# Weight sums of the second FFN product in two tiles, one filled by a copy, and DVE and ACT in text order through pairs and second product

## The chip, the core and the metric

The kernel runs on one core of a Trainium2 chip. The metric is the device time of one execution in microseconds (us). The engines that matter here: PE multiplies matrices, DVE and ACT do elementwise work, POOL issues some of the DMAs, SP issues the others. Each engine runs its instructions one after the other in the order in which they stand in its own stream; between engines, semaphores make one wait for another.

## The reference, cut to what matters

A decoder trunk of two layers in float32 on 512 tokens of width 1024. Each layer is a mixer and a feed-forward net (FFN) of width 4096 with squared ReLU:

```python
def sqrelu_mlp(x, w1, w2):
    return jnp.square(jax.nn.relu(x @ w1)) @ w2
...
    for l in range(DEPTH):
...
        x = layer_norm(DEEPNORM_ALPHA * x + mix, ln_mix_g[l], ln_mix_b[l])
        x = layer_norm(DEEPNORM_ALPHA * x + sqrelu_mlp(x, ffn_w1[l], ffn_w2[l]), ln_ffn_g[l], ln_ffn_b[l])
```

The mixers (differential and block-sparse attention in layer 0, gated linear attention in layer 1) and the norms are not touched by the change.

## The kernel before, in words

**Precision.** A float32 product is made of three products of rounded halves: each operand `v` is split into `h` (rounded copy, made by ACT, L117) and `l = v - h` (made by DVE, L118), and PE adds `h·h`, `h·l` and `l·h`. So each weight that arrives costs one ACT and one DVE instruction before PE can use it, and each step of a product is three matmuls.

**Blocks.** `ffn()` walks over the 4096 FF columns in four blocks of 1024. In each block the first matrix is done unit by unit or by pairs of units (`pair`, L872): block 0 has six plain units and one pair, blocks 1, 2 and 3 have four pairs each. Blocks 0 to 2 then multiply by their part of W2 at once (`second`, L927); block 3 is handled apart. So each layer has 13 pairs and three calls of `second`, the core 26 and six.

**A pair** replaces eight products of quarter size by seven: `b11`, `t1`, `t2`, `b21`, `t3`, `b22`, `t4`, each of 12 matmuls of 128x256 (L881), into three banks `ba`, `bb`, `bc`. Some banks are read in between and then accumulated on: ACT copies `ba` out after `b11` (`p1`, L892), `bc` after `t1` (`p5`, L896), `ba` again after `t2` (`u2`, L900). DVE then forms `c11 = p1 + bb`, `c22 = p5 + ba` (after `t3`) and `c12 = u2 + bc`, all at L815. The product `t4` accumulates on `ba`, so it may not start before `c22` has read it. Last, ACT applies ReLU and square (L914, L828, L916, L917, L828) into `hb`.

**The weights of a pair** are five entries made by `add_pair`: `first` (1024 columns), `s1` and `s2` (512), `s3` (1024), `s4` (512). `s1` is a DVE sum (L194) of a fresh load, `s2`, `s3`, `s4` are DVE subtractions (L187); each is then split. `done` hands slots back after a product and calls `pump(2)`, which writes the next entries into the text at that place.

**The second product** does seven products of 24 matmuls of 128x512 (L944) into six banks: A, C and B. Its left operands are sums of the block's activations, split into tiles `ho` by `left`. Each finished partial result is added to `x` by DVE (`into_x`, L403 and L405). Its right operands are quarters of W2: some plain loads (`raw`), some sums of two or three quarters in two `ws` tiles, built by DMAs that POOL issues (L225, and L230 for those that add to what is there).

**What sets the order.** A scheduler decides the order of each engine's stream from the program's text and its dependencies; the DMA issues of `ws` are kept in program order. The names `raw` (four buffers, loaded over SP's queue), `w` (split weights), `pp` and `pf` (PSUM banks of the first and second matrix) are those in the rows below.

Of the kernel before, what the change touches and what calls it, by code (L numbers as in the profile page):

```python
# [19 lines left out]
P = 128  # L20
# [27 lines left out]
def trunk(ctx, tc, a, out):  # L48
# [164 lines left out]
    def quad(u, i, n, half):  # L213

        return wst[u + 4 * i + 2 * n + half]
# [3 lines left out]
    def start_sums(key):  # L219

        u = blocks[key]
        tsum[key] = [t8("ws", (P, 2, 1024)) for _ in range(2)]
        for t, i in zip(tsum[key], (0, 1)):
            for half in range(2):
                tc.keep_in_program_order(nc.gpsimd.dma_start(t[:, half], quad(u, 0, 1, half)))  # L225
            for half in range(2):
                add_quad(t[:, half], quad(u, i, i, half))

# [5 lines left out]
    def add_block(u, key):  # L234
# [10 lines left out]
        def summed(m, then=None):  # L245
            def fn(half, h, l):
                t = tsum[key][m][:, half]
                split(h, l, t)
                if then:
                    add_quad(t, quad(u, *then, half))  # L250
            return [(len(loads), 2, lambda h, l, half=half: fn(half, h, l)) for half in range(2)]

        steps = (lambda: plain(0, 0), lambda: summed(0, (1, 1)), lambda: plain(1, 0), lambda: plain(1, 1),
                 lambda: summed(0, (1, 0)), lambda: summed(1), lambda: summed(0))
        return [e for st in steps for e in st()]
# [556 lines left out]
    def ffn(layer, last, nfirst, c0, t_last):  # L812
# [114 lines left out]
        def second():  # L927
# [43 lines left out]
            V.scalar_tensor_tensor(s, s, -1.0, a11, op0=ALU.mult, op1=ALU.subtract)  # L971
            V.scalar_tensor_tensor(a12, a12, -1.0, s, op0=ALU.mult, op1=ALU.subtract)
            prod("C", o1, True)
            into_x(1, 1, c["C"])
            o4 = left(a12)
            c["B"] = [bank("pf") for _ in range(2)]
            prod("B", o12, True)
            into_x(0, 0, c["B"])
            o2 = left(s)
            sub(a21, a11, a21)  # L980
            prod("C", o4, False)
            into_x(0, 1, c["C"])
            o3 = left(a21)
            prod("A", o2, False, True)
            into_x(0, 1, c["A"])
            o22 = left(a22)
# [11 lines left out]
        for b in range(NB):  # L998
# [10 lines left out]
            if b == 0:  # L1009
                third()  # L1010
            for n in range(PLAIN[b], FBLK, 2):
                pair(n // 2, ops_)
            if not fin:
                second()
                continue
# [398 lines left out]
```

## Time and profile before

| | us |
|---|---|
| median of 3 runs | 1190.36 |
| lowest, highest | 1188.38, 1193.89 |
| the profiled execution | 1192.47 |
| its span in the trace | 1190.7 |
| PE busy in it | 1140.6 (96%) |
| DVE busy | 867.8 (73%) |
| ACT busy | 622.8 (52%) |
| POOL busy | 112.2 (9%) |

The mean granted clock of TensorE in this execution is 0.992 of full speed. A busy PE is not PE at its peak: the records of matmuls overlap. So the idle time of PE, and what ended it, are what to read; the view of waits gives them by place, and the chain of work that ended last tells where the end of the execution hangs on something other than PE.

### The profile page before, as it was taken

Reading aid. Unit: us, or ns where it says so; the run is one execution under the profiler, and the core shown is the slowest. Engines: PE = TensorE matmul, PEld = TensorE weight load, DVE = VectorE, ACT = ScalarE, POOL = GpSimd, SP = SyncE. Lnnn points to the kernel's source line nnn. Section 1 sums busy time; section 2 is a strip of 40 time slices with the busy share of each in tenths; the row PEclk is TensorE's granted clock in tenths of the full one; section 3 lists DMA queues with packets and bytes.
Section 4 is the critical chain, followed back from the end, with each engine's and each line's share of the span. In section 5 each row is a group of like instructions: output and inputs, shape, how many; then the busy total and the mean of one; then the engine's idle time right before and its main releaser. Section 6 shows DMA issues by size and latency. Waiting matters only on the chain.

```text
span 1190.7 us, 16757 instructions
## 1 busy us (share of the span) xinstructions
PE 1140.6 (96%) x6538; PEld 988.1 (83%) x6538; DVE 867.8 (73%) x1359; ACT 622.8 (52%) x1046; POOL 112.2 (9%) x136
## 2 busy tenths in 40 slices
PE   9999999999989999999999999999999899899997
PEld 6787776889779789799888888888987887887986
DVE  5677863578976986995657756486879679679846
ACT  6535466446646647566336433633564565564731
POOL 1132410010110010001010000000102002000000
PEclk9999999999999999999999999999999999899998
DMA  7512242073674675435232123401656566463331
GB/s 265 205 53 71 71 147 66 1 212 94 139 210 121 141 200 142 107 106 188 72 102 84 58 87 99 138 32 50 181 159 161 140 163 174 125 168 66 121 107 71
DMA packets 42735, 145.79 MB, mean 122 GB/s; under 512 B 5152, under 2 KB 6176, under 8 KB 42656
## 3 DMA queue, kind: packets, MB, share of 16 engines
q1 hardware_dynamic: 30640, 101.92, 26.3%
q0 software_dynamic: 12016, 42.80, 16.5%
q8 instruction: 51, 0.84, 0.3%
q14 instruction: 28, 0.23, 0.1%
HBM read 142.61 MB, written 2.10 MB: 122 GB/s over the span
## 4 chain that ended last, share of the span: by engine, by line
PE 79%; DVE 6%; ACT 6%; issue 4%; DMA 3%; POOL 1%; DVEq 0%; POOLq 0%; ACTq 0%
PE pp L881 20%; PE pf L944 15%; PE pf L280 4%; PE pf L279 4%; PE pf L281 4%; PE pb L279 4%; PE pb L280 4%; PE pb L281 3%; PE pa L279 3%; PE pa L281 3%; PE pa L280 3%; DMA raw<-in_wst 3%; ACT w L117 2%; DVE w L118 2%; PE pl L1212 1%
## 5 line engine op out<-in xcount | busy, mean ns | idle before, releaser
L118 DVE TENSOR_TENSOR w<-raw,w 128x1024 fp32r<-128x1024 f32 (+2 forms) x210 | 242.6, 1165 | 122.5 <-ACT w L117 99.4
L117 ACT ACTIVATE w<-raw 128x1024 fp32r<-128x1024 f32 (+2 forms) x210 | 205.7, 986 | 167.1 <-PE pf L944 26.9
L944 PE MATMUL pf<-w,ho 128*128 128x512 f32 x1008 | 234.9, 391 | 4.9 <-ACT ho L117 4.0
L944 PEld LDWEIGHTS pf<-w,ho 128*128 128x128 f32 x1008 | 187.4, 188 | 48.0 <-ACT ho L117 6.6
L881 PE MATMUL pp<-xTh,w 128*128 128x256 f32 x832 | 161.3, 286 | 9.3 <-ACT w L117 5.8
L881 PEld LDWEIGHTS pp<-xTh,w 128*128 128x128 f32 x832 | 135.6, 194 | 12.1 <-ACT w L117 7.5
L881 PE MATMUL pp<-T,w 128*128 128x256 f32 x936 | 127.1, 289 | 14.9 <-DVE hb L815 14.9
L881 PEld LDWEIGHTS pp<-T,w 128*128 128x128 f32 x936 | 119.2, 196 | 16.8 <-DVE hb L815 15.7
L881 PE MATMUL pp<-xTl,w 128*128 128x256 f32 x416 | 118.9, 286 | 0.0
L279 PE MATMUL pa<-xTh,w 128*128 128x512 f32 x264 | 106.0, 403 | 0.0
L281 PE MATMUL pa<-xTh,w 128*128 128x512 f32 x264 | 103.1, 391 | 0.0
L280 PE MATMUL pa<-xTl,w 128*128 128x512 f32 x264 | 103.0, 390 | 0.0
L881 PEld LDWEIGHTS pp<-xTl,w 128*128 128x128 f32 x416 | 81.0, 195 | 0.2
L230 POOL DMA_DIRECT2D ws<-in_wst x48 | 42.1, 877 | 400.5 <-DVE w L118 334.8
L279 PE MATMUL pb<-w,xTh 128*128 128x512 f32 x192 | 76.3, 401 | 1.0 <-ACT w L117 1.0
L280 PE MATMUL pb<-w,xTh 128*128 128x512 f32 x192 | 75.1, 391 | 0.4 <-DVE w L118 0.4
L281 PE MATMUL pb<-w,xTl 128*128 128x512 f32 x192 | 75.3, 392 | 0.0
L117 ACT ACTIVATE w<-ws 128x1024 fp32r<-128x1024 f32 x48 | 50.8, 1059 | 42.4 <-PE pf L944 41.6
L118 DVE TENSOR_TENSOR w<-ws,w 128x1024 fp32r<-128x1024 f32 x48 | 58.1, 1220 | 14.0 <-ACT w L117 9.2
L281 PEld LDWEIGHTS pa<-xTh,w 128*128 128x128 f32 x264 | 49.6, 188 | 10.6
L280 PEld LDWEIGHTS pa<-xTl,w 128*128 128x128 f32 x264 | 49.8, 188 | 9.2
L279 PEld LDWEIGHTS pa<-xTh,w 128*128 128x128 f32 x264 | 49.7, 189 | 9.1
(280 smaller groups left out, 2082.5 us busy)
## 6 DMA issues: line engine op xcount, KB each, us to landing
raw<-in_wst SPq DMA_DIRECT2D x178, 512.0 KB, 3.6
ws<-in_wst POOLq DMA_DIRECT2D x72, 512.0 KB, 6.0
xraw<-in_xT SPq DMA_DIRECT2D x8, 256.0 KB, 4.9
x<-in_x SPq DMA_DIRECT2D x4, 512.0 KB, 6.8
gb<-in_lng POOLq DMA_DIRECT2D x4, 512.0 KB, 5.6
gb<-in_lnb POOLq DMA_DIRECT2D x4, 512.0 KB, 6.5
out_x<-x SPq DMA_DIRECT2D x7, 256.0 KB, 2.0
tab<-in_rope SPq DMA_DIRECT2D x2, 512.0 KB, 5.2
```

The costliest lines, as they stand in the source:

```text
L117: A.activation(h, src, AF.Copy)
L118: V.tensor_tensor(l, src, h.bitcast(F32), op=ALU.subtract)
L230: tc.keep_in_program_order(nc.gpsimd.dma_start(t, src, accum_op=ALU.add))
L279: PE.matmul(o, l[0], r[0], start=first, stop=False)
L280: PE.matmul(o, l[0], r[1], start=False, stop=False)
L281: PE.matmul(o, l[1], r[0], start=False, stop=last)
L881: PE.matmul(o, w[x_], z[y_], start=first and k == n == 0, stop=k == 3 and n == 2, skip_group_check=True)
L944: PE.matmul(c[k][tt], l[x_], r[y_][:, j, :], start=first and half == j == n == 0, stop=half == j == 1 and n == 2, skip_group_check=True)
L1212: PE.matmul(pl[:, h * P:(h + 1) * P], z, z, start=True, stop=True)
```

## The change

First, the two `ws` sums of a block. Before, tile 0 went through three contents (Q01+Q00, then +Q11, then +Q10) and tile 1 held Q01+Q11. Now `a1` = Q01+Q00 and `a2` starts as a copy of `a1`, made by a DMA between tiles, +Q11. After `a1` is split, it is filled anew (Q01, then +Q11); after `a2` is split, Q10 is added to it. POOL issues 14 DMAs for each block where it issued 12. Second, the products of `second` come in another order: A(Q00), C(`a1`), B(Q10), A(`a2`), C(Q11), A(`a1` anew), A(`a2`+Q10), and the left operands are formed in the order that goes with it. Third, the pairs and `second` of all blocks are put under a manual schedule for DVE and ACT: these two engines run that part in the order of the text, while PE, SP and POOL are still ordered as before.

```diff
--- before.py
+++ after.py
@@ -219,12 +219,18 @@
     def start_sums(key):
 
         u = blocks[key]
-        tsum[key] = [t8("ws", (P, 2, 1024)) for _ in range(2)]
-        for t, i in zip(tsum[key], (0, 1)):
-            for half in range(2):
-                tc.keep_in_program_order(nc.gpsimd.dma_start(t[:, half], quad(u, 0, 1, half)))
-            for half in range(2):
-                add_quad(t[:, half], quad(u, i, i, half))
+        a1, a2 = tsum[key] = [t8("ws", (P, 2, 1024)) for _ in range(2)]
+        for half in range(2):
+            bring(a1[:, half], quad(u, 0, 1, half))
+        for half in range(2):
+            add_quad(a1[:, half], quad(u, 0, 0, half))
+        for half in range(2):
+            bring(a2[:, half], a1[:, half])
+        for half in range(2):
+            add_quad(a2[:, half], quad(u, 1, 1, half))
+
+    def bring(t, src):
+        tc.keep_in_program_order(nc.gpsimd.dma_start(t, src))
 
     def add_quad(t, src):
         tc.keep_in_program_order(nc.gpsimd.dma_start(t, src, accum_op=ALU.add))
@@ -247,11 +253,16 @@
                 t = tsum[key][m][:, half]
                 split(h, l, t)
                 if then:
-                    add_quad(t, quad(u, *then, half))
+                    then(t, half)
             return [(len(loads), 2, lambda h, l, half=half: fn(half, h, l)) for half in range(2)]
 
-        steps = (lambda: plain(0, 0), lambda: summed(0, (1, 1)), lambda: plain(1, 0), lambda: plain(1, 1),
-                 lambda: summed(0, (1, 0)), lambda: summed(1), lambda: summed(0))
+        def third(t, half):
+            bring(t, quad(u, 0, 1, half))
+            add_quad(t, quad(u, 1, 1, half))
+
+        steps = (lambda: plain(0, 0), lambda: summed(0, third), lambda: plain(1, 0),
+                 lambda: summed(1, lambda t, half: add_quad(t, quad(u, 1, 0, half))),
+                 lambda: plain(1, 1), lambda: summed(0), lambda: summed(1))
         return [e for st in steps for e in st()]
 
     def add_ffn(u, layer):
@@ -969,20 +980,20 @@
             into_x(0, 0, c["A"])
             o12 = left(a12)
             V.scalar_tensor_tensor(s, s, -1.0, a11, op0=ALU.mult, op1=ALU.subtract)
-            V.scalar_tensor_tensor(a12, a12, -1.0, s, op0=ALU.mult, op1=ALU.subtract)
             prod("C", o1, True)
             into_x(1, 1, c["C"])
-            o4 = left(a12)
+            V.scalar_tensor_tensor(a12, a12, -1.0, s, op0=ALU.mult, op1=ALU.subtract)
+            o2 = left(s)
             c["B"] = [bank("pf") for _ in range(2)]
             prod("B", o12, True)
             into_x(0, 0, c["B"])
-            o2 = left(s)
+            o4 = left(a12)
             sub(a21, a11, a21)
+            prod("A", o2, False)
+            into_x(0, 1, c["A"])
+            o3 = left(a21)
             prod("C", o4, False)
             into_x(0, 1, c["C"])
-            o3 = left(a21)
-            prod("A", o2, False, True)
-            into_x(0, 1, c["A"])
             o22 = left(a22)
             prod("A", o3, False, True)
             into_x(1, 1, c["A"])
@@ -1008,10 +1019,12 @@
             fill.drain()
             if b == 0:
                 third()
-            for n in range(PLAIN[b], FBLK, 2):
-                pair(n // 2, ops_)
+            with tc.manual_schedule(engines={mybir.EngineType.DVE, mybir.EngineType.Activation}):
+                for n in range(PLAIN[b], FBLK, 2):
+                    pair(n // 2, ops_)
+                if not fin:
+                    second()
             if not fin:
-                second()
                 continue
             gb = load_gb(2 * layer + 1)
             W["un"] = 2
```

The streams of three engines show what moves. In these rows the numbers behind names are those of buffers; `w` are split weights, `s` and `raw` the unsplit sums and loads, `hb` the activations, `p1`, `p5`, `u2` the copies out of PSUM. Line 815 of before is 826 of the changed kernel, 881 is 892, and so on.

**DVE, block 1 of layer 0, second pair** (before, from the sum `s_3388` of the pair after the next to that pair's `c11`, `c22`, `c12`):

```order
L194 TENSOR_TENSOR s_3388<-raw_3123 128x512
L187 TENSOR_TENSOR raw_3040<-raw_3040,s_3261 128x512
L118 TENSOR_TENSOR w_3301<-s_3261,w_3301 128x512
L187 TENSOR_TENSOR raw_3123<-raw_3121,raw_3123 128x512
L118 TENSOR_TENSOR w_3332<-raw_3042,w_3331 128x1024
L118 TENSOR_TENSOR w_3336<-raw_3040,w_3336 128x512
L815 TENSOR_TENSOR hb_3132<-p1_3273,pp_3271 128x256
L815 TENSOR_TENSOR hb_3133<-p5_3274,pp_3270 128x256
L815 TENSOR_TENSOR hb_3132<-u2_3275,pp_3272 128x256
```

The same place in the changed kernel (raw_3044 and raw_3046 are this one's loads for the third pair, `hb_3137` and `hb_3138` the activations):

```order
L194 TENSOR_TENSOR s_3268<-raw_3046 128x512
L118 TENSOR_TENSOR w_3267<-s_3268,w_3267 128x512
L187 TENSOR_TENSOR s_3268<-s_3268,raw_3044 128x512
L118 TENSOR_TENSOR w_3308<-s_3268,w_3308 128x512
L187 TENSOR_TENSOR raw_3046<-raw_3044,raw_3046 128x512
L118 TENSOR_TENSOR w_3339<-raw_3046,w_3338 128x1024
L187 TENSOR_TENSOR raw_3044<-raw_3044,s_3268 128x512
L118 TENSOR_TENSOR w_3343<-raw_3044,w_3343 128x512
L826 TENSOR_TENSOR hb_3137<-p1_3280,pp_3278 128x256
L826 TENSOR_TENSOR hb_3138<-p5_3281,pp_3277 128x256
L826 TENSOR_TENSOR hb_3137<-u2_3282,pp_3279 128x256
```

In both, the `s3` and `s4` weights of the next loads are split ahead of `c11`, `c22` and `c12`. Before, the subtractions for them stand well ahead and the two splits follow each other; now the subtraction of `s4` (`raw_3044`) stands between the split of `s3` and that of `s4`, and the sum of a later pair (`s_3395<-raw_3127`) that stood ahead now comes behind `c12`.

**PE, the same pair** (before, the end of `t1`, then `t2` and the start of what follows it):

```order
L881 MATMUL pp_3272<-T_2573,w_3125 128x256 x12
L881 MATMUL pp_3270<-T_2574,w_3175 128x256 x12
L881 MATMUL pp_3271<-xTh_1707,w_3117 128x256
L881 MATMUL pp_3271<-xTl_1708,w_3117 128x256
L881 MATMUL pp_3271<-xTh_1707,w_3118 128x256
```

and in the changed kernel, `t2` and what follows it:

```order
L892 MATMUL pp_3277<-T_2574,w_3182 128x256 x12
L892 MATMUL pp_3279<-xTh_1707,w_3217 128x256
L892 MATMUL pp_3279<-xTl_1708,w_3217 128x256
L892 MATMUL pp_3279<-xTh_1707,w_3217 128x256 x2
L892 MATMUL pp_3277<-xTh_1707,w_3212 128x256
L892 MATMUL pp_3277<-xTl_1708,w_3212 128x256
```

`T_2574` is the right operand of `t2`. Before, `t2` is followed by the 12 matmuls of `b21` (`pp_3271`), 12 of `t3` and 12 of `b22`, and then by `t4`: 36 matmuls. Now `b21` stands ahead of `t2`, and between `t2` and `t4` lie 12 of `t3`, 12 of `b22` and four of later pairs: 28.

**ACT, the end of block 1 of layer 0** (before, from the last pair's ReLU to the operands of `second`; one half of `ho_3642` stands much earlier, in the third pair):

```order
L117 ACTIVATE w_3628<-raw_3383 128x1024
L914 ACTIVATE hb_3132<-hb_3132 128x2x256
L917 ACTIVATE hb_3133<-pp_3516 128x256
L828 ACTIVATE hb_3132<-hb_3132 128x2x256
L828 ACTIVATE hb_3133<-hb_3133 128x2x256
L117 ACTIVATE ho_3642<-hb_3132 128x512
L117 ACTIVATE w_3666<-raw_3385 128x1024
L117 ACTIVATE ho_3650<-s_3648 128x1024
```

and in the changed kernel:

```order
L117 ACTIVATE w_3637<-raw_3390 128x1024
L925 ACTIVATE hb_3137<-hb_3137 128x2x256
L839 ACTIVATE hb_3137<-hb_3137 128x2x256
L927 ACTIVATE hb_3138<-hb_3138 128x256
L928 ACTIVATE hb_3138<-pp_3523 128x256
L839 ACTIVATE hb_3138<-hb_3138 128x2x256
L117 ACTIVATE ho_3651<-hb_3137 128x512 x2
L117 ACTIVATE ho_3659<-s_3657 128x1024
```

Both halves of the first left operand (`ho_3651`) now stand together, behind the last pair's square of `hb_3138`, with the split of a raw weight (`w_3637`) ahead of the ReLU.

## Rows read from the trace of the kernel before

**Rows 1.** The page's chain that ended last: shares of the span by engine.

```profile
PE 79%; DVE 6%; ACT 6%; issue 4%; DMA 3%; POOL 1%; DVEq 0%; POOLq 0%; ACTq 0%
```

**Rows 2.** View of waits, PE, whole span: engine, line <- releaser: total us, times, longest.

```profile
PE pp L881 <- DVE hb L815: 14.9, 4, 4.3
PE pp L881 <- ACT w L117: 5.8, 4, 1.5
PE pf L944 <- ACT ho L117: 4.0, 6, 0.8
...
PE pp L881 <- DVE w L118: 3.5, 2, 1.7
...
PE pf L944 <- DVE ho L118: 0.6, 4, 0.2
```

**Rows 3.** The chain in order of time: start, us, engine and line, matmuls.

```profile
352.01 33.58 PE pp L881 x263
...
438.41 32.08 PE pp L881 x263
...
934.40 33.66 PE pp L881 x263
...
1022.13 34.50 PE pp L881 x263
```

**Rows 4.** Timeline, 344 to 352.5 us, DVE and PE: start, us, operation, [idle before <-releaser].

```profile
347.67 0.69 DVE L194 TENSOR_TENSOR s<-raw 128x512 f32<-128x512 f32 x1 [4.55 <-DMA raw<-in_wst]
...
352.01 2.93 PE L881 MATMUL pp<-T,w 128*128 128x256 f32 x12 [4.32 <-DVE hb L815]
```

**Rows 5.** Timeline where the second product of block 0 starts (PE, ACT), and 366.45 (ACT).

```profile
297.43 2.91 PE L944 MATMUL pf<-w,ho 128*128 128x512 f32 x12
...
297.51 1.06 ACT L117 ACTIVATE w<-raw 128x1024 fp32r<-128x1024 f32 x1 [1.89 <-PE pp L881]
...
298.48 0.61 ACT L914 ACTIVATE hb<-hb 128x512 f32<-128x512 f32 x1
...
299.00 0.37 ACT L917 ACTIVATE hb<-pp 128x256 f32<-128x256 f32 x1
...
300.30 0.62 ACT L117 ACTIVATE ho<-hb 128x512 fp32r<-128x512 f32 x1
...
366.45 0.62 ACT L117 ACTIVATE ho<-hb 128x512 fp32r<-128x512 f32 x1
```

**Rows 6.** Timeline, 359 to 365 us, a pair of block 1: ACT, DVE and PE.

```profile
359.35 0.38 ACT L900 ACTIVATE u<-pp 128x256 f32<-128x256 f32 x1 [0.54 <-PE pp L881]
...
359.62 1.79 ACT L117 ACTIVATE w<-raw 128x1024 fp32r<-128x1024 f32 x2
...
360.74 1.83 DVE L118 TENSOR_TENSOR w<-raw,w 128x1024 fp32r<-128x1024 f32 x2 [0.87 <-ACT w L117]
...
362.48 0.74 DVE L815 TENSOR_TENSOR hb<-p,pp 128x256 f32<-128x256 f32 x2
...
363.46 1.60 PE L881 MATMUL pp<-T,w 128*128 128x256 f32 x12
```

**Rows 7.** Groups by form, 352 to 390 us: xcount | busy us, mean ns of one.

```profile
L118 DVE TENSOR_TENSOR w<-raw,w 128x1024 fp32r<-128x1024 f32 x7 | 8.6, 1224 | 7.9 <-ACT w L117 4.1 <-PE pp L881 3.8
...
L916 ACT ACTIVATE hb<-hb 128x256 f32<-128x256 f32 x4 | 1.7, 417 | 6.6 <-DVE hb L815 6.6
...
L118 DVE TENSOR_TENSOR w<-raw,w 128x512 fp32r<-128x512 f32 x2 | 1.4, 688 | 1.2 <-ACT w L117 1.2
...
L187 DVE TENSOR_TENSOR raw<-raw,s 128x512 f32<-128x512 f32 x2 | 1.4, 682 | 0.0
L117 ACT ACTIVATE w<-raw 128x512 fp32r<-128x512 f32 x2 | 1.3, 627 | 0.1
```

**Rows 8.** Stretch table, PE: stretch, us, busy (instructions), granted clock, DMA share, GB/s.

```profile
352.00:354.00 2.00, 1.99 (x9) 0.50 0.94 305
```

**Rows 9.** The page's DMA issues: count, KB each, median us from issue to landing.

```profile
ws<-in_wst POOLq DMA_DIRECT2D x72, 512.0 KB, 6.0
```

## The prediction

> **What bounds the kernel now.** I read the chain that ended last first: 79% of it is PE [rows 1], so only what changes PE's idle time or its clock counts. Then the view of waits: in the FFN, PE stands still at two kinds of seam [rows 2]. At the six exits from `second` into the next block's pairs (three in each layer) it waits for DVE's L815 (14.9 us) and for freshly split weights (5.8 and 3.5): together 24.2. At the six starts of `second` it waits 4.0 + 0.6 for `ho`, or 0.77 each time. The reader is to see why an exit waits: PE's `t4` of a first pair begins at 352.01 after 4.32 us of idle time that L815 ended, and L815 stood in DVE's stream behind L194, the sum of a later pair, which had waited 4.55 us for its load [rows 4]. Inside a pair, PE does not wait: `u2` starts at 359.35 as `t2` ends, `c11` and `c22` end at 363.22, and `t4` follows at 363.46 with no idle time, behind 36 matmuls that kept PE busy [rows 6]. That is a narrow escape: the chain takes 3.9 us from `u2`'s start and 36 matmuls cover 36 x 0.122 = 4.4 (263 in 32.08 us at full clock [rows 3]).
>
> **Exits, removed: -24.2.** In the new DVE stream `c11`, `c22`, `c12` of a first pair stand ahead of the later pair's L194, so the wait for that load no longer holds them; the split weights of the first pair come first too. I take all 24.2 away. What is late next there is the pair's own chain, costed below, so nothing is counted as covered by it.
>
> **Starts of `second`, added: +20.0.** Before, one half of the first `ho` is split in the middle of a pair (366.45 in block 1), so PE goes on at once, at 297.43 in block 0 [rows 5]. Now both halves stand behind the last pair's tail. From the end of `t4` (T = 297.43) ACT runs the split of a raw weight, ReLU, `c21` and two squares, and reaches the second half of `ho` at 300.30, ending 0.62 later: T + 3.49 [rows 5]. The new stream has one more instruction there, ReLU of `c22`, 0.42 [rows 7] less some 0.09 by which neighbours' records overlap: T + 3.82. PE then has two matmuls before it needs the `l` half, which DVE gives 0.69 later [rows 7]: about 0.25 more. So 4.1 instead of 0.77, six times: 6 x 3.33 = 20.0. Bounds: 6 x 2.7 = 16 if the raw split ahead finds its slot early and is done by then; 6 x 3.7 = 22 if hand-overs cost as much as the 0.1 seen between T and 297.51.
>
> **Pairs, added: +43.3.** This is the large term. In the new DVE stream `c11` stands behind the `s4` weight of the next pair, and the way to it now goes back and forth: `u2` (0.38 [rows 6]), split of `s3` on ACT (1.06 [rows 5]), its `l` on DVE (1.22), the subtraction for `s4` on DVE (0.68), its split on ACT (0.63), its `l` (0.69) [rows 7], then `c11` and `c22` (0.74 [rows 6]). The sum is 5.40; records of neighbours on one engine overlap by some 0.1 and hand-overs cost about as much, so I keep 5.2 to 5.5. Before, the subtraction stood ahead and the two splits ran side by side on both engines, which is why the chain took 3.9. At the same time the cover shrinks: 28 matmuls instead of 36, 28 x 0.122 = 3.4 us. PE should wait 5.4 - 3.4 = 2.0 us at `t4`. Laid out instruction by instruction with these durations, the waits at `t4` are, in block 1: 0.6 for the first pair (24 matmuls of the last `second` product lie in between), 1.9, 2.1, 0.3 (the last pair of a block has no weights of a next one to split); in block 2: 2.2, 1.9, 2.1, 0.3; in block 3, where two splits follow each square: 2.6, 0.4, 2.8, 0.3. That is 17.5 a layer. Beside it, once in block 1 and once in block 2, the `first` weight of a later pair gets its slot only when `t4` ends, and PE's next product waits for its split and its `l`: 1.06 + 1.22 less two matmuls, 2.05 and 2.1. Together 21.65 a layer, 43.3 for two. Bounds: with every overlap of 0.1 counted and no hand-over, the chain is 4.8 and the long waits are 1.4: 0.7 of the sum, 30. With hand-overs of 0.1 at each of the four changes of engine and no overlap, 5.8: 2.4, or 52.
>
> **The last product, added: +3.3.** `o22` writes the bank that `into_x` of the product before it has to read, and this now stands in text order behind the next weights on DVE. The next pair's 48 matmuls cover most of it; I lay out 0.55 left, six times. Bounds 0 and, with one more 1.22 split ahead [rows 7], 7.
>
> **The sums in `ws`: 0.** The second contents are now formed by two transfers one behind the other instead of one, but the products that use them come later. By 6.0 us a transfer [rows 9] the later half of `a1` anew lands 17.5 us after T and is split from 23.7 on; the later half of `a2` with Q10 lands at 23.0 and is needed at 29.2. What hides them are the products between, 24 matmuls each; if that cover were too short, the price is a rival below. Two more DMAs a block on POOL's queue stand before nothing else that PE waits for. The copy between tiles isn't in the trace; I take it as a transfer like the others, 6.0, and between 2 and 9 it still lands over 30 us before its use. The other order of products keeps the number of products and of matmuls: 0.
>
> **Clock: -1.** After the idle stretch of 4.32 us the granted clock is 0.50 for two microseconds [rows 8], the lower of the two levels, 1.2 instead of 2.4 GHz, and the 263 matmuls of such a stretch take 33.58, 33.66 and 34.50 us where 32.08 is the value without a drop [rows 3]: 1.5 + 1.6 + 2.4 = 5.5 lost now, which goes with the exits' waits. The new waits at the starts of `second` are 4.1, near those that dropped the clock. I take half of the six as drops, 3 x 1.5 = 4.5, with ends 0 and 9: -5.5 + 4.5 = -1.
>
> The Trainium skill ("TensorE: Matmul & The Clock Gate", Part 1 on the HAM clock gate) says that throttled is the default, and that activity releases the clock and idleness brings the throttle back; the rows agree as far as long waits go. By that rule all six new waits could drop it, and the sum would be 4.5 higher.
>
> **The sum.** On the profiled execution: 1192.5 - 24.2 + 20.0 + 43.3 + 3.3 - 1.0 = 1233.9. That execution lies 2.1 over the median of the runs, so the forecast is 1232.
>
> **Rivals.**
> (a) *Not slower: the chain to `c22` stays hidden.* If the next pair's split weights get their slots earlier than I laid out, so that `s3` is split before `u2`, then 2.3 of the 5.4 go, the rest (3.1) is below the cover of 3.4, and PE meets no wait at `t4`. It decides at a chain of 3.4. That takes the 43.3 away: 1233.9 - 43.3 - 2.1 = 1188.5, no change. For it: before, the chain ran within its cover [rows 6]. Against it: the stream of ACT is fixed now, and `s3` stands behind `u2` in it.
> (b) *Faster: the same, and the starts hidden too.* If in addition ACT is far enough ahead that `ho` waits only for the last square, 20.0 goes: 1168. Against it: ReLU, both squares and `ho` stand one behind the other there, all behind `t4`.
> (c) *The refilled sums come late.* Three transfers in line have 6.2 us of slack; if each takes over 8.2 instead of 6.0 [rows 9], PE waits for W2. At 9.0 that is some 3 us in each of six blocks: 1232 + 18 = 1250. For it: the transfers share the DMA engines with `raw`, which had 0.94 of them busy at 352 [rows 8]. Against it: the median of 72 is 6.0.
> (d) *All starts drop the clock*: 1232 + 4.5 = 1236.
>
> **How the numbers follow.** All lower bounds together give 1192.5 - 24.2 + 16 + 30 + 0 - 5.5 - 2.1 = 1207, all upper ones 1192.5 - 24.2 + 22 + 52 + 7 + 3.5 - 2.1 = 1251. Forecast within these, with (d): 0.77, of which (d) 0.2. (a) 0.12, (b) 0.06, (c) 0.05. The range leaves out (a) and (b), 0.18. It goes down to 1197, ten below the lower bounds, for a pair term of which only 20 is left (half of it hidden, halfway to (a)), and up to 1250 by (c) and the upper bounds. A measurement of this kernel tells about 0.5% (6 us) from no change. Faster by more: (b) and a third of (a), 0.10; within: the rest of (a), 0.08; slower: 0.82.
>
> **What would show it.** Right: PE's waits at the changed L892 for L826 (was L815) number some 16 to 20 at 1.9 to 2.8 us, in the middle of blocks; waits at L955 for `ho` number six of some 4 us; none of 4 at the exits. Wrong: no waits for L826 inside blocks ((a)); PE waits for weights that come from `ws`, with a DMA behind ((c)); PE's clock below 1 after each start ((d)). The weakest step is the split of `s3` behind `u2`: if those weights are on hand earlier, the pairs cost nothing.

## The result and the profile after

The changed kernel takes 1291.8 us, median of 4 runs (1290.44 to 1293.41), beside 1191.57 of before in the same comparison: a ratio of 1.084, 95% interval 1.081 to 1.088. The direction was forecast, the size was not: 100 us came where some 42 were expected, and 1291.8 lies outside the range of 1197 to 1250.

Two figures say where the time went. Of both kernels, first before and then after, the span of the core and TensorE's mean granted clock:

```profile
core 0: 1190.7 us, clock 0.992
```

```profile
core 0: 1288.6 us, clock 0.961
```

The span grew by 97.9 us. The page's first part gives PE 1140.6 us busy before and 1184.3 after, so its idle time went from 1190.7 - 1140.6 = 50.1 to 1288.6 - 1184.3 = 104.3 us: **+54.2**. What the low clock cost can be worked out as (1 - mean clock) x span: 0.008 x 1190.7 = 9.5 before, 0.039 x 1288.6 = 50.3 after: **+40.8**. Together 95.0 of the 97.9. The formula also counts low clock while PE waits, which costs nothing; PE's busy time, for the same 6538 matmuls, grew by 1184.3 - 1140.6 = 43.7, so the order of size is right. In the kernels below the account is rougher: span less idle time less clock loss is 1131 us for before, 1134 for after, and stays within 17 of before's in all runs but the one with added matmuls. So where two kernels differ by 17 us or less, it can't divide the difference into idle time and clock.

The idle time after, by what PE waited for (view of waits, PE, whole span: engine, line <- releaser: total us, times, longest). It answers [rows 2]:

```profile
PE pf L955 <- ACT ho L117: 24.1, 6, 4.1
PE pp L892 <- DVE hb L826: 18.9, 11, 2.2
PE pp L892 <- ACT w L117: 17.7, 10, 2.5
PE pp L892 <- ACT p L903: 7.8, 6, 1.4
PE pf L955 <- DVE x L414: 7.1, 6, 1.3
PE pf L290 <- ACT w L117: 4.7, 2, 2.4
...
PE pp L892 <- DVE w L118: 2.8, 6, 0.8
```

The six waits for `ho` are there, 24.1 us where before had 4.0. None of the 4 us waits at an exit is left. But PE now waits inside the pairs for `hb`, for split weights (from ACT's L117 and from DVE's L118) and for `p1`, and in the last product for `into_x` (L414).

The low clock, first behind a wait in the second pair of block 1 of layer 0 (PE's timeline: start, us, operation, [idle before <-releaser]; then start:end, us, PE busy (instructions), granted clock, DMA share, GB/s), beside [rows 8]:

```profile
360.57 2.25 PE L892 MATMUL pp<-T,w 128*128 128x256 f32 x12 [2.16 <-DVE hb L826]
```

```profile
360.00:361.00 1.00, 0.43 (x3) 1.00 0.82 291
361.00:362.00 1.00, 1.00 (x9) 0.72 0.86 164
362.00:368.00 6.00, 4.35 (x18) 0.50 0.15 61
368.00:370.00 2.00, 2.00 (x17) 0.93 0.00 0
```

PE waited 2.16 us up to 360.57 for `c22` and began the 12 matmuls of `t4`; within them the clock fell to the lower of the two levels, 1.2 GHz. The waits of 1.19 us for a weight and of 0.46 for its `l`, at 364.02 and 365.28, came when it was already low. So a single wait went before this drop, and it is shorter than the 3.86 to 4.32 us that dropped the clock before. In the next pair a wait of 1.53 us alone, up to 377.00, was followed by a drop too:

```profile
376.00:378.00 2.00, 1.00 (x6) 1.00 0.65 244
...
379.00:381.00 2.00, 2.00 (x11) 0.50 0.42 166
```

Length alone does not decide: after 2.54 us (up to 465.40 in this kernel) and 2.62 us (up to 438.41 in before) the clock stayed at 1.00. The 10 us around the end of each of the six waits for `ho`, in the same columns:

```profile
303.00:313.00 10.00, 9.08 (x34) 0.83 0.79 205
405.00:415.00 10.00, 8.10 (x24) 0.66 0.62 159
507.00:517.00 10.00, 8.13 (x23) 0.66 0.64 157
934.00:944.00 10.00, 7.41 (x22) 0.66 0.63 174
1039.00:1049.00 10.00, 9.38 (x33) 0.83 0.68 181
1142.00:1152.00 10.00, 8.03 (x23) 0.66 0.61 160
```

All six starts dropped the clock. By (1 - clock) x 10 they lost 1.7 or 3.4 us each, 17.0 together. In the whole trace the clock record has 18 stretches at 0.50 ahead of the last microseconds: these six, and twelve behind waits in the pairs and at the end of block 3, eleven of those behind a single wait of 1.5 to 2.6 us.

### The profile page after: what moved, and what is told of

Read it like the earlier page. It is cut to its first block, busy times and chain, and to the rows that moved or that the text cites. A ratio compares the mean times of both kernels' runs of the same rounds, so it can differ in the third digit from the quotient of the medians.

```text
span 1288.6 us, 16761 instructions
## 1 busy us (share of the span) xinstructions
PE 1184.3 (92%) x6538; PEld 1018.8 (79%) x6538; DVE 872.3 (68%) x1359; ACT 630.2 (49%) x1046; POOL 119.3 (9%) x148
## 5 line engine op out<-in xcount | busy, mean ns | idle before, releaser
L118 DVE TENSOR_TENSOR w<-raw,w 128x1024 fp32r<-128x1024 f32 (+2 forms) x210 | 244.0, 1166 | 168.6 <-ACT w L117 163.7
L117 ACT ACTIVATE w<-raw 128x1024 fp32r<-128x1024 f32 (+2 forms) x210 | 204.4, 987 | 230.3 <-DVE raw L187 69.7
L955 PE MATMUL pf<-w,ho 128*128 128x512 f32 x1008 | 246.3, 407 | 31.2 <-ACT ho L117 24.1
L955 PEld LDWEIGHTS pf<-w,ho 128*128 128x128 f32 x1008 | 197.8, 198 | 77.1 <-ACT ho L117 25.4
L892 PE MATMUL pp<-xTh,w 128*128 128x256 f32 x832 | 177.2, 297 | 20.8 <-ACT w L117 17.7
L892 PE MATMUL pp<-T,w 128*128 128x256 f32 x936 | 146.4, 307 | 27.0 <-DVE hb L826 18.9
L892 PEld LDWEIGHTS pp<-xTh,w 128*128 128x128 f32 x832 | 142.9, 201 | 28.8 <-ACT w L117 19.9
L892 PEld LDWEIGHTS pp<-T,w 128*128 128x128 f32 x936 | 132.5, 211 | 33.5 <-DVE hb L826 21.1
L892 PE MATMUL pp<-xTl,w 128*128 128x256 f32 x416 | 119.7, 290 | 0.0
L892 PEld LDWEIGHTS pp<-xTl,w 128*128 128x128 f32 x416 | 83.2, 200 | 0.5
L117 ACT ACTIVATE w<-s 128x512 fp32r<-128x512 f32 x52 | 32.7, 629 | 88.8 <-DVE s L194 60.4
L118 DVE TENSOR_TENSOR w<-ws,w 128x1024 fp32r<-128x1024 f32 x48 | 58.0, 1218 | 20.7 <-ACT w L117 19.8
L117 ACT ACTIVATE w<-ws 128x1024 fp32r<-128x1024 f32 x48 | 50.3, 1060 | 44.0 <-PE pf L955 41.8
L118 DVE TENSOR_TENSOR w<-s,w 128x512 fp32r<-128x512 f32 x52 | 36.0, 692 | 44.6 <-ACT w L117 44.6
L233 POOL DMA_DIRECT2D ws<-in_wst x24 | 15.1, 632 | 495.8 <-DVE w L118 261.3
L292 PEld LDWEIGHTS pa<-xTh,w 128*128 128x128 f32 x264 | 49.6, 188 | 10.6
```

The source lines that it names most:

```text
L117: A.activation(h, src, AF.Copy)
L118: V.tensor_tensor(l, src, h.bitcast(F32), op=ALU.subtract)
L233: tc.keep_in_program_order(nc.gpsimd.dma_start(t, src))
L292: PE.matmul(o, l[1], r[0], start=False, stop=last)
L892: PE.matmul(o, w[x_], z[y_], start=first and k == n == 0, stop=k == 3 and n == 2, skip_group_check=True)
L955: PE.matmul(c[k][tt], l[x_], r[y_][:, j, :], start=first and half == j == n == 0, stop=half == j == 1 and n == 2, skip_group_check=True)
```

## The experiments

All ratios are to before, run on the same chip beside each kernel; before itself had medians of 1191.57 to 1195.13 us.

| kernel | median us | ratio [95%] | PE idle | mean clock | clock loss |
|---|---|---|---|---|---|
| before | 1191.57 | 1 | 50.1 | 0.992 | 9.5 |
| after | 1291.8 | 1.084 [1.081, 1.088] | 104.3 | 0.961 | 50.3 |
| e1 new sums and products alone | 1177.0 | 0.986 [0.982, 0.991] | 35.6 | 0.992 | 9.4 |
| e2 text order alone | 1314.7 | 1.104 [1.099, 1.108] | 113.3 | 0.951 | 64.3 |
| e3 text order in `second` alone | 1180.1 | 0.990 [0.986, 0.994] | 35.3 | 0.992 | 9.4 |
| e4 text order in pairs alone | 1237.3 | 1.038 [1.035, 1.042] | 66.3 | 0.974 | 32.1 |
| e5 waits filled with zeros | 1274.8 | 1.069 [1.065, 1.073] | 73.4 | 0.991 | 11.5 |
| e6a weights behind `c22` | 1321.4 | 1.108 [1.103, 1.112] | 124.7 | 0.946 | 71.2 |
| e6b `ho` early | 1275.1 | 1.069 [1.065, 1.074] | 101.4 | 0.979 | 26.8 |
| e6 both | 1331.6 | 1.117 [1.113, 1.121] | 138.1 | 0.944 | 74.5 |
| e7 DVE alone in text order | 1222.2 | 1.023 [1.017, 1.029] | 61.8 | 0.984 | 19.5 |
| e8 ACT alone in text order | 1213.7 | 1.016 [1.010, 1.021] | 58.1 | 0.981 | 23.1 |
| e9 before, `o2` by halves | 1193.0 | 1.000 [0.997, 1.003] | 45.0 | 0.988 | 14.3 |
| e10 `l` behind the next subtraction | 1224.9 | 1.025 [1.021, 1.030] | 62.4 | 0.983 | 20.8 |
| e11 e10 and `ho` early | 1214.4 | 1.017 [1.014, 1.020] | 57.3 | 0.994 | 7.3 |
| e12 before, new order of products | 1171.2 | 0.980 [0.977, 0.984] | 30.9 | 0.998 | 2.3 |
| e13 e1 with e10's text | 1175.9 | 0.984 [0.980, 0.987] | 35.7 | 0.992 | 9.4 |
| e14 e3 with e10's text | 1172.1 | 0.982 [0.979, 0.985] | 29.7 | 0.994 | 7.0 |
| e15 e14 with old tiles | 1170.3 | 0.981 [0.977, 0.985] | 30.2 | 0.997 | 3.5 |
| e16 after with old tiles | 1292.1 | 1.083 [1.078, 1.088] | 106.9 | 0.961 | 50.3 |

### Which part of the change

e1 takes the manual schedule away (`second` and the pairs as in before, outside the `with`), e2 is before with it:

```diff
-            with tc.manual_schedule(engines={mybir.EngineType.DVE, mybir.EngineType.Activation}):
-                for n in range(PLAIN[b], FBLK, 2):
-                    pair(n // 2, ops_)
-                if not fin:
-                    second()
+            for n in range(PLAIN[b], FBLK, 2):
+                pair(n // 2, ops_)
+            if not fin:
+                second()
```

> The changed kernel without the manual schedule: the new sums, the copy between tiles and the new order of products stay. Theory (the order of DVE and ACT makes PE wait, and the waits let the granted clock fall): t2 is followed by 36 matmuls again and one half of ho is split early again, so PE idles about as before; 1185 to 1198 us, clock 0.99. Rival (the refilled sums come late or the longer chain of DMAs is the cost): most of the 100 us stay, 1240 us or more, with PE waiting at L955 for weights that come from ws.

> The kernel before with the manual schedule alone: old sums, old order of products. Theory: nearly the whole loss, 1280 to 1300 us, clock 0.96, waits for ho of 24 us and for L815 of some 19. Rival (sums): 1190 to 1220 us.

e1 measured 1177.0, e2 1314.7. So the loss lies in the text order, and the sums with their order of products are a gain, of 16 us where DVE and ACT are free (1193.2 for before on that chip, 1177.0 for e1) and of 1314.7 - 1291.8 = 23 under text order. Both sizes are outside what I had written (e1 below its range, e2 above).

e3 and e4 put the `with` around `second` alone or around the pairs alone.

> The changed kernel with the manual schedule around the second product alone; the pairs are free, and one half of ho moves into the pairs again. Theory: the waits inside pairs and at the starts are gone; 1188 to 1205 us, clock 0.98 or more. Rival (the order of DVE inside the second product holds back into_x and the weights): PE waits inside the second product, 1230 us or more.

> The changed kernel with the manual schedule around the pairs alone. One half of ho moves into the pairs again, so the six waits of 4.0 us for ho go; the waits for L826 and for split weights inside pairs stay. Theory: idle time falls by some 20 us, and with it some of the clock's loss: 1240 to 1262 us, clock 0.97. Rival (the starts of the second product carry the clock's loss alone): clock back at 0.99, 1215 to 1230 us.

e3 measured 1180.1, under its range: text order inside `second` costs some 3 us over e1, less than either kernel's runs spread. e4 measured 1237.3, just under its range, and not for the reason given: the waits for `ho` did not go. Two rows of its view of waits:

```profile
PE pf L955 <- ACT ho L117: 20.8, 6, 3.7
...
PE pp L892 <- DVE hb L826: 2.0, 2, 1.0
```

Its 20.8 us for `ho` (after: 24.1) remain, and the waits for `hb` shrink to 2.0. e4 costs 60 us over e1 and e3 costs 3, but both under one schedule cost 115. A possible reason is that the pairs then enter the text order with their first weights bound to the place where `second` writes them, behind its `into_x`; no run tests it.

e7 and e8 put DVE alone or ACT alone in text order:

> The changed kernel with DVE alone in text order; ACT is free. Theory (in text order DVE takes turns with ACT: each entry's subtraction, ACT's split, DVE's l, then the next entry, so a pair's weights take some 13 us where PE needs 84 x 0.122 = 10.3): the turn-taking stays, as DVE's stream still has each l ahead of the next entry's subtraction; 1225 to 1275 us, and DVE's idle time before L118 that ACT ended stays above 150 us. Rival (ACT's order is what holds PE back, by u2 and ho): 1175 to 1205 us.

> The changed kernel with ACT alone in text order; DVE is free. Theory (turn-taking in DVE's stream): DVE's subtractions move ahead again, t2 is followed by 31 or 36 matmuls; most of the loss goes, 1180 to 1215 us. Rival (ACT's order): 1240 us or more.

They measured 1222.2 and 1213.7, 45 and 37 us over e1, and together (after) 115. e8 is inside its expected range; e7 lies just under its own, and the idle time of the page's largest L118 group that ACT ended was 122.1 us there, not over 150. So neither engine's order alone gives the whole loss. What each gives can be read from two rows of e8, beside after's 24.1 and 18.9:

```profile
PE pf L955 <- ACT ho L117: 24.0, 6, 4.1
PE pp L892 <- DVE hb L826: 9.3, 4, 3.4
```

ACT's order alone brings the whole wait at the starts, and little in the pairs: 9.3 us for `hb` is what e1 has too (9.6). So e8's 37 us, idle 58.1 - 35.6 = 22.5 and clock 23.1 - 9.4 = 13.7, are about the price of the starts. In e7 the pairs are slow: from one `c11` to the next it takes 13.8 and 11.8 us in block 1, where e8 takes 9.3 and 11.1 (DVE's L826 in their timelines).

### The clock

In e5 PE gets matmuls of zeros to run while it waits:

```diff
+        def idle_for(o, n):
+            for _ in range(n):
+                PE.matmul(o[:, :P], still, still, start=False, stop=True, skip_group_check=True)
...
             prod(ba, w, 0, "t3", False)
+            idle_for(ba, 20)
             add(c22, p5, ba)
...
             prod(ba, w, 1, "t4", False)
+            if p == 3 and not st["fin"]:
+                idle_for(ba, 36)
             done(w)
```

> The changed kernel with extra matmuls of zeros on PE where it waits: 20 of 128x128 between t3 and c22 in each pair, and 36 after t4 of a block's last pair. They add zero to banks that hold the same sums after them, so they do no useful work; PE runs them in time that it would spend waiting for DVE and ACT, or that lengthens the path where it does not wait. Theory (the granted clock falls because PE idles): the clock rises to 0.98 or more and the time falls by 15 to 40 us, to 1250 to 1277 us, although PE does more. Rival (something else lowers the clock, or the clock's loss lies in time that is hidden): the time stays or rises, 1290 to 1305 us, clock 0.96.

Measured: 1274.8 us, clock 0.991. The added group as its row shows it (line, engine, operation, count | busy us, mean ns | idle before), and two of the waits that remain:

```profile
L887 PE MATMUL pp<-still 128*128 128x128 bf16 x736 | 46.7, 219 | 0.0
```

```profile
PE pf L964 <- ACT ho L119: 12.0, 6, 2.1
...
PE pp L898 <- DVE hb L828: 7.7, 10, 1.0
```

PE does 46.7 us of work more and the kernel is 17 us faster. The waits are filled, so that those for `ho` and `hb` go from 43.0 to 19.7 us, and the clock loss falls from 50.3 to 11.5. So it is the idle stretches that take the clock down. The pairs stay slow at full clock: from one `c11` to the next it still takes 15.2 and 12.5 us in block 1 (359.74, 374.94 and 387.45, DVE's L828), with a clock of 1.00 from 350 to 400; PE needs 10.3 for a pair at full clock, and 1.3 for the 20 added matmuls (20 x 46.7 / 736). Only a part of after's slowness there is the clock.

### What PE waits for in the pairs

My theory in the prediction was one chain: `c22` stands behind the `s4` weight. e6a moves the weights behind `c22`, e6b writes the first `ho` early, e6 does both:

```diff
             prod(bb, w, 1, "b21", True)
-            done(w)
+            release(w[0])
             add(c11, p1, bb)
             w = nxt()
             prod(ba, w, 0, "t3", False)
             add(c22, p5, ba)
+            pump(2)
```

```diff
+            if p == 3 and not st["fin"]:
+                st["o11"] = h, l = [t4("ho", (P, 4, 256), F32R) for _ in range(2)]
+                split(h[:, :2], l[:, :2], H[0][:, 0, :2])
             p1, p5, u2 = t1("p1"), t1("p5"), t1("u2")
...
             prod(ba, w, 1, "t4", False)
-            done(w)
+            release(w[0])
             r = H[0][:, :, p, :]
             A.activation(r, r, AF.Relu)
             square(0, p)
+            if p == 3 and not st["fin"]:
+                h, l = st["o11"]
+                split(h[:, 2:], l[:, 2:], H[0][:, 0, 2:])
+            pump(2)
```

> The changed kernel with one edit in the text of a pair: the next weights (s3, s4) are written behind c11 and c22 and not ahead of them; DVE and ACT still run in text order. Theory (c22 waits behind the chain of s3 and s4 weights): PE's 18.9 us of waits for L826 fall under 5, and the time to 1255 to 1278 us. Rival (DVE and ACT are simply late throughout): PE waits as long for the weights that now come later; 1285 to 1300 us.

> The changed kernel with one half of the first ho written ahead of the last pair, the other half right behind the square that makes it, and the weights that t4 sets free behind that; DVE and ACT still run in text order. Theory (the six waits of 4.0 us for ho cost themselves and a low clock after each): waits for ho fall from 24.1 to under 6 us, time to 1240 to 1265 us. Rival (what is moved behind is then late by as much): 1280 us or more.

> Both edits of the text together, DVE and ACT still in text order. Theory: both kinds of waits are gone and the clock is near 0.99; 1195 to 1235 us. Rival (late weights take their place): 1260 us or more.

e6a measured 1321.4 us, 30 slower than after and above both its ranges; e6 measured 1331.6, on its rival's side, with 54.3 us of waits for weights. The waits of e6a:

```profile
PE pp L892 <- ACT w L117: 31.2, 12, 3.3
PE pp L892 <- ACT p L903: 26.3, 6, 6.1
...
PE pp L892 <- DVE hb L826: 1.0, 2, 0.5
```

The wait for `hb` is gone (1.0 of 18.9 us), and the weights are late instead: 31.2 + 26.3 us for `w` and `p` where after had 17.7 + 7.8. The rival's account was right, though the loss was larger than it said, and my theory of one chain fell: PE would have waited for DVE and ACT anyway. e6b measured 1275.1: 17 us less, but its idle time hardly changed (101.4); the starts' long waits became shorter ones in other places and the clock loss halved. It missed its range, and with 21.7 us in 12 waits for `ho` also the 6 us that I had given for them.

A new theory came from the timeline of after around the third pair of block 1, first DVE, then two rows of ACT (start, us, operation, [idle before <-releaser]):

```profile
359.77 0.74 DVE L826 TENSOR_TENSOR hb<-p,pp 128x256 f32<-128x256 f32 x2
...
376.64 0.74 DVE L826 TENSOR_TENSOR hb<-p,pp 128x256 f32<-128x256 f32 x2
...
377.64 1.22 DVE L118 TENSOR_TENSOR w<-raw,w 128x1024 fp32r<-128x1024 f32 x1
378.77 0.68 DVE L194 TENSOR_TENSOR s<-raw 128x512 f32<-128x512 f32 x1
380.21 0.69 DVE L118 TENSOR_TENSOR w<-s,w 128x512 fp32r<-128x512 f32 x1 [0.76 <-ACT w L117]
380.94 0.69 DVE L187 TENSOR_TENSOR s<-s,raw 128x512 f32<-128x512 f32 x1
383.42 0.69 DVE L118 TENSOR_TENSOR w<-s,w 128x512 fp32r<-128x512 f32 x1 [1.79 <-ACT w L117]
384.03 0.69 DVE L187 TENSOR_TENSOR raw<-raw 128x512 f32<-128x512 f32 x1
387.30 1.23 DVE L118 TENSOR_TENSOR w<-raw,w 128x1024 fp32r<-128x1024 f32 x1 [2.59 <-ACT w L117]
388.45 0.69 DVE L187 TENSOR_TENSOR raw<-raw,s 128x512 f32<-128x512 f32 x1
389.83 0.69 DVE L118 TENSOR_TENSOR w<-raw,w 128x512 fp32r<-128x512 f32 x1 [0.69 <-ACT w L117]
390.44 0.74 DVE L826 TENSOR_TENSOR hb<-p,pp 128x256 f32<-128x256 f32 x2
```

```profile
385.94 0.38 ACT L911 ACTIVATE u<-pp 128x256 f32<-128x256 f32 x1 [2.28 <-PE pp L892]
386.22 1.05 ACT L117 ACTIVATE w<-raw 128x1024 fp32r<-128x1024 f32 x1
```

Four of the five rows of L118 wait for ACT's split of the same entry, and each sum or subtraction (L194, L187) stands behind the L118 of the entry before. So DVE and ACT take turns: from 377.64 to 391.2 DVE works 8.0 us and waits 0.76 + 1.79 + 2.59 + 0.69 = 5.8 us. The longest of these waits holds ACT's own wait of 2.28 us for PE's `t2`, since the split of `s3` stands behind `u2` there: a late pair makes the next weights late. From 376.64 to 390.44, one `c11` to the next, it is 13.8 us, and from 359.77 to 376.64 16.9; PE needs 84 matmuls x 0.122 [rows 3] = 10.3 for a pair at full clock. Not all of that is the hand-over: the 16.9 holds the stretch at 0.50 shown above, and without the 2.28 us of waiting for PE the 13.8 would be some 11.5, by estimate, still more than 10.3. Over the whole span the largest group of weight splits on DVE, first before, then after, has this idle time (after the second |; last, what ACT ended):

```profile
L118 DVE TENSOR_TENSOR w<-raw,w 128x1024 fp32r<-128x1024 f32 (+2 forms) x210 | 242.6, 1165 | 122.5 <-ACT w L117 99.4
```

```profile
L118 DVE TENSOR_TENSOR w<-raw,w 128x1024 fp32r<-128x1024 f32 (+2 forms) x210 | 244.0, 1166 | 168.6 <-ACT w L117 163.7
```

The same 210 instructions are as long; they wait 64 us more for ACT. e10 tests it: text order stays, but where one call writes two entries, the `l` of the first is written behind the sum or subtraction of the second (loads are issued at the end of the call):

```diff
+    def flush():
+        while pend:
+            h, l, src = pend.pop(0)
+            V.tensor_tensor(l, src, h.bitcast(F32), op=ALU.subtract)
+
+    def later(h, l, src):
+        flush()
+        A.activation(h, src, AF.Copy)
+        pend.append((h, l, src))
...
         def s3(h, l):
             a1, a2 = got[u], got.pop(u + 1)
             sub(a2[:, :512], a1[:, :512], a2[:, :512])
-            split(h, l, a2)
+            later(h, l, a2)
 
         def s4(h, l):
             a12 = got.pop(u)[:, 512:]
             sub(a12, a12, st.pop("s"))
-            split(h, l, a12)
+            later(h, l, a12)
```

> The changed kernel with DVE and ACT still in text order, but the text of a pair's weights written so that the l of one entry stands behind the next entry's sum or subtraction where one call writes two entries (first with s1, s3 with s4). Same instructions, same number. Theory (turn-taking): two of the five hand-overs of a pair are covered by 0.68 us of DVE work each, some 1.4 us less per pair for some 18 pairs, 25 us of PE's idle time and about as much again of the clock's loss: 1235 to 1262 us. Rival (c22 stands behind the s4 weight, whose chain from u2 is hardly shorter, or the starts carry the loss): 1275 to 1295 us.

It measured 1224.9, 67 us less than after and 10 under the range that I had given. `c11` of the second, third and fourth pair of block 1, and what PE still waits for:

```profile
358.04 0.74 DVE L846 TENSOR_TENSOR hb<-p,pp 128x256 f32<-128x256 f32 x2
...
369.79 0.75 DVE L846 TENSOR_TENSOR hb<-p,pp 128x256 f32<-128x256 f32 x2
...
380.55 0.75 DVE L846 TENSOR_TENSOR hb<-p,pp 128x256 f32<-128x256 f32 x2
```

```profile
PE pf L975 <- ACT ho L117: 24.0, 6, 4.1
...
PE pp L912 <- ACT p L923: 4.0, 4, 1.1
PE pp L912 <- ACT w L155: 2.5, 4, 0.9
PE pp L912 <- DVE hb L846: 2.4, 8, 0.6
```

From pair to pair it is now 11.75 and 10.76 us in this block, near PE's 10.3 (in block 3 still 12.9 and 12.3), and the waits inside pairs are 4.0 + 2.5 + 2.4 = 8.9 us where after had 47.2 for the same rows. The waits for `ho` are untouched. The gain is larger than the 1.4 us per pair that I had worked out: 16.9 + 13.8 became 11.75 + 10.76, 4 us a pair. The wait of 2.28 us for `u2` suggests why it can be more, since lateness of PE comes back to ACT, and the clock is higher: in e10's clock record the FFN has low stretches behind the six starts alone. No run divides the two. Loads are also issued somewhat later here; with the same text and a free scheduler (e13, below) that gained nothing.

e11 takes the starts away as well:

> e10 with the first ho written early as in e6b; DVE and ACT in text order. Theory (each start costs 4.0 us of idle time and a low clock after it): the 24.0 us of waits for ho fall under 8 us and the clock rises above 0.985; 1190 to 1208 us. Rival (as in e6b, what is put behind makes the pairs or ho's second half late): 1212 us or more, with new waits for ho or L846.

It measured 1214.4, the rival's side: the waits for `ho` fell from 24.0 to 14.3 us only, and those for weights rose from 2.5 to 9.0. Both idle time (62.4 to 57.3) and clock loss (20.8 to 7.3) fell, together by more than the 10 us gained, so the account doesn't divide this gain.

### What the sums and products gain

e9 is before with `prod("A", o2, False)`; e12 is before with the new order of products and operands but the old contents of the tiles; e16 is after, e15 is e14, each with the old contents.

```diff
         steps = (lambda: plain(0, 0), lambda: summed(0, (1, 1)), lambda: plain(1, 0), lambda: plain(1, 1),
                  lambda: summed(0, (1, 0)), lambda: summed(1), lambda: summed(0))
+        steps = (lambda: plain(0, 0), lambda: summed(0, (1, 1)), lambda: plain(1, 0),
+                 lambda: summed(0, (1, 0)), lambda: plain(1, 1), lambda: summed(1), lambda: summed(0))
```

> The kernel before with one of the changed kernel's details alone: the fifth product of second (operand o2) takes its two weights one after the other and not both at once for each half of the tokens, so their slots come free earlier. If this is why the new sums alone gained some 14 us (the waits of 5.8 and 3.5 us for split weights at the exits go, and part of the 14.9): 1176 to 1185 us. Rival (the gain lies in the two tiles' contents or in the order of products): 1187 to 1195 us.

> The kernel before with the changed kernel's order of products (fourth A with o2, fifth C with o4) but the old contents of the two ws tiles and 12 DMAs a block; DVE and ACT free. If the order of products and of the left operands is what gained: 1172 to 1182 us, and no waits for split weights at the exits. If it is the tiles' contents: 1187 to 1195 us.

> The changed kernel with the old contents of the ws tiles (no copy, 12 DMAs a block) under the new order of products; DVE and ACT in text order for pairs and second. If the contents cost or save nothing: the changed kernel's 1292 us within 5. If they matter under text order: 1275 to 1285 us, or 1300 us and more.

e9 measured 1193.0, no change. e12 measured 1171.2, a ratio of 0.980. e16 measured 1292.1 beside 1291.8. So under text order the contents of the tiles, the copy and the two more DMAs cost and save nothing. With DVE and ACT free, e12 is 6 us below e1, which has the new contents, but the intervals of their ratios overlap. The order of products alone brings the gain of e1. e12 lies just under the range written for it, without waits for split weights as written there. The wait of e12, beside the 24.2 us of [rows 2] at the exits:

```profile
PE pp L881 <- DVE hb L815: 5.3, 4, 1.6
```

The waits for split weights at the exits are gone, and those for L815 fall from 14.9 to 5.3 us. Why is seen in part only: DVE's wait at L194 for a load, which stood ahead of `c11` in [rows 4], falls over the span from 17.1 (six times) to 7.9 us (four times):

```profile
DVE s L194 <- DMA raw<-in_wst: 17.1, 6, 4.6
```

```profile
DVE s L194 <- DMA raw<-in_wst: 7.9, 4, 2.3
```

Why the loads come earlier was not followed further.

### Faster versions

> e1 (no manual schedule, new sums) with the pairs' weights written as in e10. Theory (turn-taking costs only under text order, since a free scheduler moves the subtractions ahead anyway): the same as e1 within 1%, 1168 to 1186 us. Rival (the scheduler keeps much of the text's order): 10 us or more below e1, 1165 us or less.

> e3 (manual schedule around second alone) with the pairs' weights written as in e10; entries for the next pairs that are written inside second come in text order. Theory: the waits of 7.2 us for split weights of e3 get smaller, 1170 to 1182 us. Rival: no difference from e3's 1180 us, or slower, as l stands later for the pair that needs it at once.

> e14 (manual schedule around second alone, weights of pairs written as in e10) with the old contents of the ws tiles, 12 DMAs a block and no copy. If the contents cost nothing: e14's 1172 us within 4. If the copy and the refill cost something where the order is the same: 1160 to 1168 us.

e13 measured 1175.9, e14 1172.1, e15 1170.3. e13 is e1 within its spread: where a scheduler is free, the turn-taking is not there to be taken away. e14 is 8 us below e3; e15 equals e14. e12, e14 and e15 lie some 2% below before and cannot be told from each other; e12 is the smallest edit.

## Why the prediction was right and wrong

**Exits (-24.2).** Right in size, with half of the cause. None of the long waits at exits is left in after. Text order alone (e2) does take the waits of about 4 us for L815 away, as the prediction argued, and leaves waits for split weights at the exits:

```profile
PE pp L881 <- DVE hb L815: 19.1, 12, 2.2
...
PE pp L881 <- DVE w L118: 9.1, 12, 1.3
```

The new order of products, which the prediction put at nothing, removes these, and by itself takes the 24.2 to 5.3 us (e12).

**Starts (+20.0).** Right: 24.1 instead of 4.0 us for `ho`, 4.0 to 4.1 each, and in e8 by ACT's order alone. The chain from `t4` through the weight split, ReLU, squares and `ho` is as it was worked out.

**Pairs (+43.3 of idle time).** Near in size by luck, wrong in mechanism. The rows of PE's waits at L892 for `hb`, `w`, `p` and `l`, 18.9 + 17.7 + 7.8 + 2.8 = 47.2 us, and 4.7 for the weights at the end of block 3, are 51.9. The parts did not come as laid out: the waits at `t4` for `hb`, laid out at 2 x 17.5 = 35, are 18.9 (11 waits, eight of about 2 us, where 16 to 20 were to show it), and those for weights, laid out at 8.3, are 25.2. The step held one chain, from `u2` through `s3` and `s4` to `c22`, as a wait that comes once a pair against a fixed cover. e6a took that wait away and the kernel got slower. The limit is one of rate: in text order DVE and ACT take turns, so in block 1 the middle pairs take 13.8 to 16.9 us, and 12.5 to 15.2 with the clock restored (e5), where PE needs 10.3; with the turns shortened they take 10.8 to 11.8, and the kernel is 67 us faster (e10). The prediction had the durations for it and compared them with 28 matmuls instead of with a pair. Waits for `p1`, 7.8 us, were not in it at all.

**The last product (+3.3).** Twice the size: 7.1 us, six waits of up to 1.3; the upper bound was 7.

**Sums (0).** Right for the tiles and the copy under text order: `ws` transfers landed in 6.1 us and the copy in 4.4, and e16 equals after. Wrong for the order of products: -24 us in e12 (1195.1 to 1171.2).

**Clock (-1).** This is the step that failed. It measured +40.8. The prediction let only the six starts count, half of them, at 1.5 us each, and put the clock behind the waits inside the pairs at nothing without a reason, though it forecast many waits of about 2 us there. In the rows of before, waits of 3.86 us and more dropped the clock while one of 2.62 did not. In after all six starts dropped it, at 1.7 or 3.4 us each (17.0 instead of 4.5), and waits of 1.5 to 2.6 us in the pairs did so too. With the 5.5 of the exits gone, 40.8 + 5.5 - 17.0 = 29.3 is left, by estimate, for those waits. With the terms as measured, idle +54.2 and clock +40.8, the sum is 1192.5 + 95.0 - 2.1 = 1285, within 7 us of the result. The prediction's idle terms, -24.2 + 20.0 + 43.3 + 3.3 = 42.4, were 12 us short; the clock was 42 short.

The Trainium skill ("TensorE: Matmul & The Clock Gate", Part 1) says that activity releases the throttle, and that idleness brings it back. The runs agree: e5 puts activity of no use into the idle stretches, and the mean clock goes from 0.961 to 0.991. The prediction used that sentence for the long waits only.

**Rivals.** (a) and (b) did not come; (d), all starts dropping the clock, came and cost more than its price, but is the smaller part of the clock's loss; (c) did not: PE met no wait at L955 for weights. (Its limit, 6.0 + 6.2 / 3, is 8.1 and not 8.2.)

## What to carry to other kernels

When two engines hand each piece of work back and forth, compare the time that one whole unit takes them, hand-overs counted, with the time that the bottleneck engine needs for that unit; the single wait that e6a removed only moved. If an order is written by hand, write the dependent second half of a piece behind the first half of the next, since a free scheduler did just that here and text order undid it. And price new idle time of PE with its clock, behind waits of about 2 us too. There is no fixed rate here: over before, after lost 40.8 us of clock to 54.2 of idle time, e8 13.6 to 8.0, e6b 17.3 to 51.3, and e11 nothing to 7.2.

## What the runs showed of the hardware that I had not expected

Single waits of 1.5 to 2.6 us were followed by the lower level of the granted clock, as those of 4 us were (0.50 behind 2.16 and behind 1.53 in after), while 2.54 in after and 2.62 in before were not; what decides between them no run here shows. And matmuls of zeros that fill waits can be worth more than they cost: 736 of them, 46.7 us busy, in the pairs and at the starts, made the kernel 17 us faster.
